# Recurrent scan of a two-layer RWKV and attention network: a new table of hops, finer pieces, a longer pipeline, and the state's identity product in two corners

## The chip, the cores and the metric

The kernel runs on one core of a Trainium2 chip, in one launch. The metric is the device time in microseconds of an execution; lower is better. All arithmetic is in float32; PE is TensorE, DVE is VectorE, ACT is ScalarE, POOL is GpSimd, SP is SyncE.

## The reference, cut to what matters

Two layers over 256 context rows and 256 latent rows of 1024 channels: layer 0 is an RWKV-7 mixer, layer 1 global attention, each between two gated feed-forward halves. The change touches the recurrence of layer 0 alone. It runs over 16 heads of 64 channels, in two directions, first over the context rows and then, from the state reached, over the latent rows:

```python
def rwkv_scan(state0, dd, reverse):
    def step(s, inp):
        r_t, w_t, k_t, v_t, a_t, b_t = inp
        sa = jnp.einsum('bhvk,bhk->bhv', s, a_t)
        s = s * w_t[:, :, None, :] + sa[..., None] * b_t[:, :, None, :] + v_t[..., None] * k_t[:, :, None, :]
        return s, jnp.einsum('bhvk,bhk->bhv', s, r_t)
    xs = tuple(jnp.moveaxis(dd[nm], 1, 0) for nm in ('r', 'decay', 'k', 'v', 'a', 'b'))
    s_fin, ys = lax.scan(step, state0, xs, reverse=reverse)
    return s_fin, jnp.moveaxis(ys, 0, 1)
```

Each direction's `y` is then normalised per head, scaled, gated and added (the readout).

## The kernel before, in words

The program goes through the network stage by stage; weights are split into two float32r parts so that one product becomes three matmuls. Before the scan a features stage writes, for each of eight channel tiles (128 channels, two heads), the scan's inputs to DRAM; the scan (`rwkv_scan`, from L885) reads them back. It works in chunks of 64 rows: four chunks per half (`hf` 0 is the context, 1 the latent rows), eight steps per tile, both directions `d` and both heads `h` side by side.

A tile goes through four generators. `produce` (L930) makes the chunk matrices in pieces: `scores` (products of `bk` and `ar` on PE, masked by DVE at L951), `keys` (transposes of `bk`, evicted by ACT at L991) and `values` (transposes of `v`, evicted by ACT at L974 and L975). What a piece evicts is put on the list `late` and issued one hop later. `solve` (L997) inverts the small triangular blocks on DVE, some forty instructions in a chain; `couple` (L1032) joins the inverses to 64 rows with four rounds of 32*32 products (`first` twice, `third`, `fourth`, each for two halves `hf`), with DVE and ACT moving the results between (`refine`, `turn`, `diagonal`, `corner`). `scan` (L1135) has three hops per step: A forms `rp` (L1149, and L1156 with the state S) and ACT evicts it as `rt` (L1160), with `past` (L1126) adding the state's part of the output; B forms `up` from `rt` (L1167), evicted by ACT in two halves to `uv`; C forms the new state `sp` from an identity product of S (L1175) and the products of `bkt` and `uv` (L1181), which ACT evicts and scales by `pc` (L1186), and the output `yp` (L1192). `readout` (L1204) follows a half.

The order of all this is written out by hand: the instructions of each engine run in the order in which the program issues them, within a hop the running scan first, then tile by tile, the oldest first. The table `plan` (L94) says at which hop t, counted from a tile's own start, each thing is issued. A tile starts every P = 24 hops, so up to three tiles are under way. PIECES gives the hops of the twelve pieces (four scores, four keys, four values), SOLVE the start of the solve and RATE its instructions per hop, COUPLE the couple's hops, SCAN the start of the scan, SS and BC (modulo 24) two parts of the readout, BK the loads of the next tile's `pc`, `ar` and `bk`, V those of the own `v`, LOADS those of `ax` and `r`. All these loads but tile 0's, and the readout's, go through POOL's queue (`ldq`), in program order too, beside POOL's memsets of `uv`.

Buffers: `ar` and `v` come from a pool of two (one per half), `pc` from a pool of three (`m3`), `bkt` and `uv` from one of four; `bk` is two fixed tiles `bks`, `ax` and `tt` two fixed tiles each. A write into a buffer waits for the last read of its last owner, wherever that read stands in the program. `pc` of a tile is read by L1186 in hop C of steps 0 to 6. PSUM banks for pieces, couple and readout come from one pool of five.

The lines that carry the order:

```python
                for z in reversed(live[:]):
                    if hop - z[0] >= pl["SCAN"] and not adv(z[5]):
                        live.remove(z)
```

Of the kernel before, what the change touches and what calls it, by code (L numbers as in the profile page):

```python
# [12 lines left out]
ALU = mybir.AluOpType  # L13
# [74 lines left out]
class Net:  # L88


    def __init__(self, ctx, tc, a):
        self.ctx, self.tc, self.nc, self.a = ctx, tc, tc.nc, a
        self.last = {}
        self.plan = dict(  # L94
            P=24, SOLVE=12, RATE=6, COUPLE=range(24, 32), SCAN=32,
            PIECES=(0, 3, 6, 9, 8, 11, 16, 18, 12, 14, 20, 21),
            END={(0, 0): (5, (3, 3)), (0, 1): (5, (3, 3)), (1, 0): (5, (3, 3))}, WO=(4, 4), NI=(5, 5),
            FST=(1, 3), WAIT=16, RH=0, FB=16, CLEAR=(14, 18), AS=1, BK=(11, 20), V=(5, 13), LOADS=(21, 33), SS=(21, 10), BC=(1, 14))
        nc = self.nc
        self.res = ctx.enter_context(tc.tile_pool(name="res", bufs=1))  # L100
        self.dram = ctx.enter_context(tc.tile_pool(name="dram", bufs=1, space=DRAM))
        self.vec = self.res.tile([128, NV, KT], F32, name="vec")
        self.cst = self.res.tile([128, NC], F32, name="cst")
        self.ones = self.res.tile([128, 128], F32, name="ones")
        cv = self.res.tile([128, KT, 2], F32, name="cv")
        self.cs = self.res.tile([128, KT, 32], F32, name="cs")
        self.mod = [self.res.tile([128, NMOD, KT, 2], F32, name=f"mod{l}") for l in range(2)]
        self.epsn = self.res.tile([128, 1], F32, name="epsn")
        self.epsg = self.res.tile([128, 1], F32, name="epsg")
        self.xsp = self.dram.tile([128, 2, KT, CTX], F32, name="xsp")  # L110
        nc.sync.dma_start(out=cv, in_=a["cv"])
# [773 lines left out]
    def rwkv_scan(self):  # L885
        nc, a, tc = self.nc, self.a, self.tc
        with ExitStack() as st:
# [12 lines left out]
            def load(ct, hf, ldq=nc.gpsimd):  # L900

                z = zs.setdefault(ct, {})
                if hf == 0:
                    z["pc"] = m3.tile([128, 2, 8], F32, tag="pc", name="pc")
                    ldq.dma_start(out=z["pc"], in_=self.fpc[ct])
                z["bk", hf] = bks[hf]
                z["ar", hf] = e2.tile([128, 2, 4, 2, 64], F32, tag="ar", name="ar")
                ldq.dma_start(out=z["ar", hf].rearrange("p d c s i -> p (d c s i)"), in_=self.far[ct, :, hf].rearrange("p d x -> p (d x)"))
                ldq.dma_start(
                    out=bks[hf].rearrange("p d c x -> p (d c x)"), in_=self.fbk[ct, :, hf].rearrange("p c s i -> p (c s i)"))  # L910

            def load_v(ct, hf):
                z = zs[ct]
# [16 lines left out]
            def produce(ct):  # L930
# [4 lines left out]
                def after(f):  # L935

                    late.append(f)

                def scores(hf, d):

                    bk, ar = z["bk", hf], z["ar", hf]
                    p = [psc.tile([128, 4, 128], F32, tag="sc", name="scp") for _ in range(2)]
                    for c in range(4):
                        for h in range(2):
                            q = 64 * h
                            nc.tensor.matmul(  # L946
                                out=p[h][:, c], lhsT=bk[q:q + 64, d, c], rhs=ar[q:q + 64, d, c].rearrange("p s i -> p (s i)"),
                                start=True, stop=True, tile_position=(q, 0))

                    def f(h):  # L950
                        nc.vector.tensor_tensor(out=sc[:, hf, d, :, h], in0=p[h], in1=mask, op=ALU.mult)  # L951
                        if h == 0:
                            after(lambda: f(1))
                    after(lambda: f(0))

                def values(hf, d):

# [21 lines left out]
                def keys(hf, h):  # L979
# [7 lines left out]
                    for d in range(2):  # L987
# [2 lines left out]
                                p[:, d, c], bk[q:q + 64, d, c], idn[q:q + 64, q:q + 64])  # L990
                    after(lambda: nc.scalar.activation(out=bkt[:, :, :, h], in_=p, func=AF.Copy))  # L991

                return [lambda g=g, hf=hf, e=e: g(hf, *e)
                        for g, es in ((scores, ((0,), (1,))), (keys, ((0,), (1,))), (values, ((0,), (1,))))
                        for hf in range(2) for e in es]

            def solve(ct):  # L997

# [6 lines left out]
                for q in range(0, 128, 32):  # L1005
                    src = sca[q:q + 32, :, 1 - q // 64, q % 64:q % 64 + 32]
                    nc.vector.transpose(out=ext[q:q + 32], in_=src.rearrange("p u (j t) -> p t u j", j=2))
                    yield q == 96
                    yield
                xl = m1.tile([128, 16, 16], F32, tag="xl", name="xl")  # L1010
                nc.vector.scalar_tensor_tensor(
                    out=xl, in0=ext[:, :, 0:16], scalar=m[0], in1=ext[:, :, 16:32], op0=ALU.mult, op1=ALU.add)
# [19 lines left out]
            def couple(ct):  # L1032
# [5 lines left out]
                def ublock(u, q, h, c0):  # L1038
                    return z["sc"][q:q + 32, u // 8, u // 4 % 2, u % 4, h, c0:c0 + 32]
# [14 lines left out]
                def half(t, hf):  # L1054
                    return t[:, 8 * hf:8 * hf + 8]
# [2 lines left out]
                qt = m1.tile([128, 16, 32], F32, tag="qt", name="qt")  # L1058
                wd = m1.tile([128, 16, 32], F32, tag="wd", name="wd")
                p = [None, None]  # L1060
                nc.vector.transpose(out=tn, in_=td)
                p[0] = first(0, lambda u, q: ublock(u, q, 1 - q // 64, q % 64), tn)
                yield
                p[1] = first(1, lambda u, q: ublock(u, q, 1 - q // 64, q % 64), tn)
                nc.vector.tensor_tensor(out=half(qt, 0), in0=half(tn, 0), in1=p[0], op=ALU.add)
                yield
                nc.vector.tensor_tensor(out=half(qt, 1), in0=half(tn, 1), in1=p[1], op=ALU.add)
                p[0] = first(0, lambda u, q: qt[q:q + 32, u], td)
                yield
                p[1] = first(1, lambda u, q: qt[q:q + 32, u], td)  # L1070

                def refine(hf):
                    nc.vector.scalar_tensor_tensor(
                        out=half(wd, hf), in0=half(td, hf), scalar=2.0, in1=p[hf], op0=ALU.mult, op1=ALU.subtract)
                    nc.vector.transpose(out=half(tn, hf), in_=half(wd, hf))

                refine(0)
                yield
                refine(1)

                def third(hf):
                    p[hf] = bank()
# [8 lines left out]
                    nc.scalar.activation(out=half(qt, hf)[32:64], in_=p[hf][32:64], func=AF.Copy)  # L1091
                    nc.vector.tensor_copy(out=half(qt, hf)[96:128], in_=p[hf][96:128])

                def diagonal(hf):
                    for q in range(0, 128, 32):
                        nc.scalar.activation(out=tt[q:q + 32, hf, :, q:q + 32], in_=half(wd, hf)[q:q + 32], func=AF.Copy)

                def fourth(hf):
                    p[hf] = bank()
# [7 lines left out]
                def corner(hf):  # L1107
                    nc.scalar.activation(out=tt[64:96, hf, :, 96:128], in_=p[hf][64:96], func=AF.Copy, scale=-1.0)
                    nc.vector.tensor_scalar(out=tt[0:32, hf, :, 32:64], in0=p[hf][0:32], scalar1=-1.0, scalar2=None, op0=ALU.mult)

                third(0)
                third(1)
                yield
                turn(0)
                turn(1)
                diagonal(0)
                yield
                fourth(0)
                fourth(1)
                yield  # L1120
                corner(0)
                corner(1)
                diagonal(1)
                yield

            def past(yp, S, r, c):  # L1126
# [8 lines left out]
            def scan(ct):  # L1135
                z = zs[ct]
                S = None
                for i in range(8):
# [33 lines left out]
                    if i < 7:  # L1172
                        sp = ps_.tile([128, 2, 64], F32, tag="s", name="sp")
                        if S is not None:
                            nc.tensor.matmul(  # L1175
                                out=sp.rearrange("p d e -> p (d e)"), lhsT=idn, rhs=S.rearrange("p d e -> p (d e)"),
                                start=True, stop=False, skip_group_check=True)
                        for d in range(2):
                            for h in range(2):
                                q = 64 * h  # L1180
                                nc.tensor.matmul(  # L1181
                                    out=sp[q:q + 64, d], lhsT=bkt[:, d, c, h], rhs=uv[:, d, c, h], start=S is None and d == 0, stop=True,
                                    tile_position=(0, q), skip_group_check=True)
                        sn = l2.tile([128, 2, 64], F32, tag="S", name="S")
                        for d in range(2):
                            nc.scalar.activation(out=sn[:, d], in_=sp[:, d], func=AF.Copy, scale=z["pc"][:, d, i:i + 1])  # L1186
# [58 lines left out]

            zs, reads = {}, []
            ldq = nc.gpsimd
            tts, bks, axs = [], [], []
            for i in range(2):
                bks.append(e2.tile([128, 2, 4, 128], F32, tag="bk", name="bk"))  # L1250
            for i in range(2):
                tts.append(l2.tile([128, 2, 8, 128], F32, tag="tt", name="tt"))
                axs.append(l2.tile([128, 2, 4, 2, 64], F32, tag="ax", name="ax"))
# [23 lines left out]
            while hop < P * KT or live or reads:  # L1277
# [10 lines left out]
                for t0, c, pr, so, co, sn in live:  # L1288
# [11 lines left out]
                        drain(so)  # L1300
                    if t in pl["COUPLE"]:
                        adv(co)
                    for i in [i for i, at in enumerate(pl["PIECES"]) if at == t]:
                        pr[i]()
                    for hf in range(2):
                        if t == pl["BK"][hf] and c + 1 < KT:
                            load(c + 1, hf)
# [285 lines left out]
```

## Time and profile before

| | us |
|---|---|
| three runs | 2365.75, 2373.47 (median), 2376.3 |
| profiled execution | 2373.17 |
| its span, first to last instruction | 2371.4 |
| stage of the scan in it, from the first loads to the last readout | 752 to 1130 |
| stages before / after it | 752 / 1241 |

The profile is of one execution. Its times count from the first instruction; a group of rows gives busy time, a timeline the start and the duration of each instruction or run of equal instructions, and in brackets how long the engine stood idle before it and which engine's instruction ended that. A PE row counts two instructions for each float32 product. Matmul ends are modelled, so starts are the better measure.

### The profile page before, as it was taken

To read this page: it belongs to the slowest core of one execution; us is meant where nothing else is said; L and a number is where in the kernel's file an instruction comes from. 1 tells how busy PE (TensorE), PEld (TensorE's weight loads), DVE (VectorE), ACT (ScalarE), POOL (GpSimd) and SP (SyncE) were. 2 spreads that over 40 slices of the span, in tenths; PEclk is the share of its full clock that TensorE was granted. 3 is DMA by queue.
4 is the path that set the end of the run, shared out by engine and by line. 5 is a ranking of instruction groups with operands and counts; after the bars stand their busy time and mean duration, and the time that the engine had idled before them with its cause. 6 is when DMAs were issued, how large, how long until landed. Compare 5 with 4: busy or idle time off the path is not lost.

```text
span 2371.4 us, 44667 instructions
## 1 busy us (share of the span) xinstructions
PE 2188.6 (92%) x18452; PEld 1875.9 (79%) x18452; DVE 1517.2 (64%) x2609; ACT 1077.5 (45%) x1944; POOL 182.6 (8%) x273
## 2 busy tenths in 40 slices
PE   7999999888996799898899999999999999998997
PEld 4777889666774688777888788998878898678997
DVE  3798336576886657663699833479983367775554
ACT  3322225445883445454663222464222355555443
POOL 0000000000453223221000000000000000000000
PEclk9999999898998779998999999999999999798999
DMA  7577336442676434332567633567763364103554
GB/s 257 194 220 225 96 105 191 149 133 82 228 249 208 116 96 120 97 96 72 181 205 243 192 98 91 162 190 231 231 209 92 113 177 136 59 12 122 180 180 138
DMA packets 103051, 366.25 MB, mean 154 GB/s; under 512 B 13008, under 2 KB 15424, under 8 KB 100160
## 3 DMA queue, kind: packets, MB, share of 16 engines
q1 hardware_dynamic: 85536, 300.35, 40.7%
q0 software_dynamic: 17312, 63.05, 8.4%
q8 instruction: 145, 2.38, 0.4%
q14 instruction: 58, 0.48, 0.1%
HBM read 330.78 MB, written 32.57 MB: 153 GB/s over the span
## 4 chain that ended last, share of the span: by engine, by line
PE 49%; DVE 11%; issue 6%; ACT 5%; DMA 5%; POOL 1%; DVEq 0%; SPq 0%; ACTq 0%; POOLq 0%
PE h L261 5%; PE h L259 5%; PE h L260 5%; PE yps L261 4%; PE yps L259 4%; PE yps L260 4%; DMA y<-in_modt 3%; DVE junk L213 3%; DVE wlo L252 2%; PE scp L946 2%; PE op L1457 1%; PE cpl L1049 1%; PE sp L1181 1%; DMA fgl<-yx 1%; PE yo L261 1%
## 5 line engine op out<-in xcount | busy, mean ns | idle before, releaser
L251 ACT ACTIVATE whi<-wp 128x1024 fp32r<-128x1024 f32 (+1 forms) x396 | 409.2, 1034 | 738.8 <-PE h L260 389.9
L252 DVE TENSOR_TENSOR wlo<-wp,whi 128x1024 fp32r<-128x1024 f32 (+1 forms) x396 | 471.9, 1192 | 382.5 <-ACT whi L251 378.7
L261 PE MATMUL h<-nh,wlo 128*128 128x512 f32 (+1 forms) x1520 | 525.2, 347 | 18.3 <-DVE wlo L252 18.0
L259 PE MATMUL h<-nh,whi 128*128 128x512 f32 (+1 forms) x1520 | 523.8, 345 | 8.1 <-ACT whi L251 6.3
L260 PE MATMUL h<-nh,whi 128*128 128x512 f32 (+1 forms) x1520 | 522.8, 344 | 0.0
L261 PEld LDWEIGHTS h<-nh,wlo 128*128 128x128 f32 x1520 | 290.0, 191 | 63.2 <-DVE wlo L252 29.4
L259 PEld LDWEIGHTS h<-nh,whi 128*128 128x128 f32 x1520 | 290.4, 191 | 42.1 <-ACT whi L251 7.9
L260 PEld LDWEIGHTS h<-nh,whi 128*128 128x128 f32 x1520 | 290.4, 191 | 33.6
L261 PE MATMUL yps<-hid,wlo 128*128 128x256 f32 (+1 forms) x1034 | 314.2, 304 | 1.9 <-DVE wlo L252 1.9
L259 PE MATMUL yps<-hid,whi 128*128 128x256 f32 (+1 forms) x1034 | 314.2, 304 | 0.0
L260 PE MATMUL yps<-hid,whi 128*128 128x256 f32 (+1 forms) x1034 | 313.9, 304 | 0.0
L261 PEld LDWEIGHTS yps<-hid,wlo 128*128 128x128 f32 x1034 | 197.4, 191 | 10.7 <-DVE wlo L252 2.8
L260 PEld LDWEIGHTS yps<-hid,whi 128*128 128x128 f32 x1034 | 197.5, 191 | 7.9
L259 PEld LDWEIGHTS yps<-hid,whi 128*128 128x128 f32 x1034 | 197.5, 191 | 7.7
L213 DVE SCALAR_TENSOR_TENSOR junk<-y 128x1024 bf16<-128x1024 f32 x144 | 176.1, 1223 | 20.6 <-DMA y<-in_modt 18.6
L404 DVE TENSOR_TENSOR gg<-s,h 128x512 f32<-128x512 f32 (+1 forms) x98 | 56.0, 572 | 95.1 <-PE h L261 93.1
L213 DVE SCALAR_TENSOR_TENSOR junk<-dw,cb 128x1024 bf16<-128x1024 f32 x80 | 97.9, 1224 | 13.5 <-DMA dw<-in_modt 10.2
L406 ACT ACTIVATE hid<-gg 128x512 fp32r<-128x512 f32 (+1 forms) x98 | 52.3, 534 | 111.4 <-DVE gg L404 111.2
L261 PE MATMUL pp<-hid,wlo 128*128 128x512 f32 x232 | 92.5, 400 | 7.0 <-DVE wlo L252 6.8
L259 PE MATMUL pp<-hid,whi 128*128 128x512 f32 x232 | 93.0, 401 | 4.2 <-ACT whi L251 4.2
L260 PE MATMUL pp<-hid,whi 128*128 128x512 f32 x232 | 91.9, 396 | 0.0
L951 DVE TENSOR_TENSOR sc<-scp,cst 128x512 f32<-128x512 f32 x64 | 42.8, 685 | 31.2 <-PE scp L946 31.0
(306 smaller groups left out, 3536.5 us busy)
## 6 DMA issues: line engine op xcount, KB each, us to landing
wp<-in_w SPq DMA_DIRECT2D x243, 512.0 KB, 3.6
wp<-in_w SPq DMA_DIRECT2D x94, 448.0 KB, 3.4
y<-in_modt SPq DMA_DIRECT2D x72, 512.0 KB, 4.4
dw<-in_modt SPq DMA_DIRECT2D x40, 512.0 KB, 4.2
wp<-in_wrkv SPq DMA_DIRECT2D x40, 512.0 KB, 4.0
mw<-in_modw SPq DMA_DIRECT2D x32, 512.0 KB, 4.9
far<-ar POOLq DMA_DIRECT2D x8, 1024.0 KB, 5.9
ar<-far POOLq DMA_DIRECT2D x14, 512.0 KB, 5.0
```

The costliest lines, as they stand in the source:

```text
L213: nc.vector.scalar_tensor_tensor(out=junk, in0=ws[i % len(ws)], scalar=1.0, in1=cb[:, s], op0=ALU.mult, op1=ALU.mult, accum_out=self.mod[l ...
L251: nc.scalar.activation(out=hi, in_=raw, func=AF.Copy)
L252: nc.vector.tensor_tensor(out=lo, in0=raw, in1=hi.bitcast(F32), op=ALU.subtract)
L259: nc.tensor.matmul(out=ps, lhsT=wh, rhs=vh, start=first and j == 0, stop=False)
L260: nc.tensor.matmul(out=ps, lhsT=wh, rhs=vl, start=False, stop=False)
L261: nc.tensor.matmul(out=ps, lhsT=wl, rhs=vh, start=False, stop=last and j == n - 1)
L404: nc.vector.tensor_tensor(out=gg, in0=s1, in1=ps[1], op=ALU.mult)
L406: nc.scalar.activation(out=hi, in_=gg, func=AF.Copy)
L946: nc.tensor.matmul(out=p[h][:, c], lhsT=bk[q:q + 64, d, c], rhs=ar[q:q + 64, d, c].rearrange("p s i -> p (s i)"), start=True, stop=True, t ...
L951: nc.vector.tensor_tensor(out=sc[:, hf, d, :, h], in0=p[h], in1=mask, op=ALU.mult)
L1049: nc.tensor.matmul(out=p[q:q + 32, u], lhsT=lhs(8 * hf + u, q), rhs=rhs[q:q + 32, 8 * hf + u], start=True, stop=True, tile_position=(q, q))
L1181: nc.tensor.matmul(out=sp[q:q + 64, d], lhsT=bkt[:, d, c, h], rhs=uv[:, d, c, h], start=S is None and d == 0, stop=True, tile_position=(0, ...
```

## The change

The plan gets new hops. The pieces are named (`s` scores, `k` keys, `v` values; half, then direction or head; for scores also which two of four chunks) and placed in a table FILL. Scores are cut in two; the couple takes eleven hops where it took eight, with at most one round's half on PE and one `diagonal` copy (now by 32-row strip over both halves, four where there were eight) in each; the scan starts at t = 41 where it started at 32. `bk` comes from the pool of four, and the next tile's loads are issued at t = 6 and 9. The solve yields once per strip transpose. The identity product is issued as two products of 64 rows and 64 columns.

```diff
-            P=24, SOLVE=12, RATE=6, COUPLE=range(24, 32), SCAN=32,
-            PIECES=(0, 3, 6, 9, 8, 11, 16, 18, 12, 14, 20, 21),
+            P=24, SOLVE=14, RATE=5, COUPLE=range(30, 41), SCAN=41,
+            FILL={0: ("s000", "s001"), 1: ("s010",), 2: ("s011",), 3: ("s100", "s101"), 4: ("s110",), 5: ("s111",), 15: ("k00",),
+                  16: ("v00",), 17: ("v01",), 19: ("k01",), 20: ("k10",), 21: ("k11",), 22: ("v10",), 23: ("v11",)},
...
-            FST=(1, 3), WAIT=16, RH=0, FB=16, CLEAR=(14, 18), AS=1, BK=(11, 20), V=(5, 13), LOADS=(21, 33), SS=(21, 10), BC=(1, 14))
+            FST=(1, 3), WAIT=16, RH=0, FB=16, CLEAR=(14, 18), AS=1, BK=(6, 9), V=(8, 14), LOADS=(30, 42), SS=(6, 18), BC=(10, 22))
...
-                z["bk", hf] = bks[hf]
+                z["bk", hf] = m4.tile([128, 2, 4, 128], F32, tag="bk", name="bk")
...
-                    p = [psc.tile([128, 4, 128], F32, tag="sc", name="scp") for _ in range(2)]
-                    for c in range(4):
+                    if part == 0:
+                        z["ps"] = [psc.tile([128, 4, 128], F32, tag="sc", name="scp") for _ in range(2)]
+                    p = z["ps"]
+                    for c in (2 * part, 2 * part + 1):
...
-                def diagonal(hf):
-                    for q in range(0, 128, 32):
-                        nc.scalar.activation(out=tt[q:q + 32, hf, :, q:q + 32], in_=half(wd, hf)[q:q + 32], func=AF.Copy)
+                def diagonal(q):
+                    nc.scalar.activation(
+                        out=tt[q:q + 32].rearrange("p f u t -> p (f u) t")[:, :, q:q + 32], in_=wd[q:q + 32], func=AF.Copy)
...
+                nc.vector.transpose(out=tn, in_=td)
+                yield
+                p[0] = first(0, lambda u, q: ublock(u, q, 1 - q // 64, q % 64), tn)
+                yield
+                p[1] = first(1, lambda u, q: ublock(u, q, 1 - q // 64, q % 64), tn)
+                nc.vector.tensor_tensor(out=half(qt, 0), in0=half(tn, 0), in1=p[0], op=ALU.add)
+                yield
+                p[0] = first(0, lambda u, q: qt[q:q + 32, u], td)
+                nc.vector.tensor_tensor(out=half(qt, 1), in0=half(tn, 1), in1=p[1], op=ALU.add)
+                yield
+                p[1] = first(1, lambda u, q: qt[q:q + 32, u], td)
+                refine(0)
+                yield
                 third(0)
+                refine(1)
+                yield
                 third(1)
                 turn(0)
+                diagonal(0)
+                yield
+                fourth(0)
                 turn(1)
+                diagonal(32)
+                yield
                 fourth(1)
                 corner(0)
+                diagonal(64)
+                yield
                 corner(1)
+                diagonal(96)
                 yield
...
-                            nc.tensor.matmul(
-                                out=sp.rearrange("p d e -> p (d e)"), lhsT=idn, rhs=S.rearrange("p d e -> p (d e)"),
-                                start=True, stop=False, skip_group_check=True)
+                            for q in (0, 64):
+                                nc.tensor.matmul(
+                                    out=sp[q:q + 64].rearrange("p d e -> p (d e)"), lhsT=idn[q:q + 64, q:q + 64],
+                                    rhs=S[q:q + 64].rearrange("p d e -> p (d e)"),
+                                    start=True, stop=False, tile_position=(q, q), skip_group_check=True)
```

## Rows read from the trace of the kernel before

**Rows 1.** Stretches: start:end, length, busy per engine, granted clock, DMA share, GB/s.

```profile
752.00:798.30 46.30, 25.21 (x601) 23.60 (x602) 25.56 (x62) 15.45 (x27) 11.42 (x19) 0.61 0.49 139
798.30:841.80 43.50, 40.47 (x930) 35.22 (x931) 24.92 (x64) 21.15 (x65) 12.86 (x21) 0.81 0.34 101
841.80:887.00 45.20, 41.68 (x948) 36.02 (x947) 27.57 (x70) 21.82 (x68) 12.85 (x21) 0.86 0.36 103
887.00:930.10 43.10, 39.72 (x940) 34.44 (x940) 27.59 (x70) 21.77 (x67) 12.86 (x21) 0.88 0.36 104
930.10:970.00 39.90, 35.72 (x940) 30.71 (x940) 27.67 (x70) 21.81 (x67) 12.86 (x21) 1.00 0.39 118
970.00:1011.40 41.40, 37.55 (x940) 32.27 (x940) 27.35 (x70) 21.80 (x67) 12.85 (x21) 0.96 0.36 106
1011.40:1051.40 40.00, 35.79 (x940) 30.71 (x940) 27.59 (x70) 21.79 (x67) 15.23 (x26) 1.00 0.41 119
1051.40:1094.80 43.40, 36.77 (x884) 31.45 (x884) 24.43 (x65) 21.79 (x67) 7.50 (x11) 0.87 0.29 89
1094.80:1122.20 27.40, 26.33 (x370) 22.00 (x372) 6.20 (x14) 11.27 (x42) 1.27 (x2) 0.77 0.05 17
```

**Rows 2.** Timeline, PE and ACT, at the end of the period that closes at 1051.4.

```profile
1049.21 1.69 ACT L1096 ACTIVATE tt<-wd 32x256 f32<-32x256 f32 x4
...
1049.30 0.71 PE L989 MATMUL btp<-cst,bk 64*128 64x64 f32 x8
...
1051.74 0.45 PE L1167 MATMUL up<-rt,tt 128*64 128x64 f32 x8 [1.73 <-ACT rt L1160]
```

**Rows 3.** Stretches (columns as in rows 1): one early, two around that point.

```profile
830.70:854.60 23.90, 23.84 (x354) 21.32 (x354) 13.15 (x27) 10.82 (x33) 6.66 (x11) 0.50 0.23 70
...
1045.00:1052.60 7.60, 5.39 (x142) 4.61 (x140) 3.85 (x8) 6.46 (x19) 6.15 (x10) 1.00 0.53 154
1052.60:1062.80 10.20, 10.20 (x120) 9.15 (x118) 7.51 (x15) 3.55 (x13) 0.00 (x0) 0.50 0.01 5
```

**Rows 4.** Waits of PE from 798.3 to 1094.8: total us, times, longest.

```profile
PE cpl L1049 <- issue: 4.6, 6, 1.8
```

**Rows 5.** Timeline of PE, 996.8 to 1003.4, at full clock.

```profile
997.47 0.45 PE L1149 MATMUL rp<-uv,sc 128*64 128x64 f32 x8
...
998.08 0.45 PE L1131 MATMUL yp<-r,S 64*64 64x64 f32 x8
998.46 0.72 PE L1049 MATMUL cpl<-td,qt 32*32 32x32 f32 x60
...
1001.11 1.16 PE L946 MATMUL scp<-ar,bk 64*128 64x128 f32 x16
1002.20 0.49 PE L1175 MATMUL sp<-S,cst 128*128 128x128 f32 x2
1002.62 0.45 PE L1181 MATMUL sp<-uv,bkt 128*64 128x64 f32 x8
1002.90 0.40 PE L1192 MATMUL yp<-sc,uv 128*64 128x64 f32 x8
1003.24 0.34 PE L1086 MATMUL cpl<-tn,sc 32*32 32x32 f32 x10
```

**Rows 6.** The page's costliest groups: DVE's masking of the scores.

```profile
L951 DVE TENSOR_TENSOR sc<-scp,cst 128x512 f32<-128x512 f32 x64 | 42.8, 685 | 31.2 <-PE scp L946 31.0
```

**Rows 7.** Timeline of POOL from 926 to 1012, one of six like it.

```profile
964.05 1.39 POOL L924 DMA_DIRECT2D ax<-far  x2 [15.18 <-PE rp L1156]
...
966.30 0.57 POOL L905 DMA_DIRECT2D pc<-fpc  x1
```

**Rows 8.** Timeline of ACT behind rows 5: both evictions of the state.

```profile
1003.18 0.52 ACT L1186 ACTIVATE S<-sp,pc 128x64 f32<-128x64 f32 x2 [2.07 <-PE sp L1181]
```

**Rows 9.** The tile v, 790 to 1060: its loads.

```profile
DMA to landing us min/median/max: 3.2/5.0/6.8
```

**Rows 10.** DMA issues, 851 to 866: KB each, median us to landing.

```profile
v<-fv POOLq DMA_DIRECT2D x2, 256.0 KB, 6.6
```

More of the change, by code (lines that the diff above doesn't have):

```diff
@@ L909, in load @@
                 ldq.dma_start(
-                    out=bks[hf].rearrange("p d c x -> p (d c x)"), in_=self.fbk[ct, :, hf].rearrange("p c s i -> p (c s i)"))
+                    out=z["bk", hf].rearrange("p d c x -> p (d c x)"), in_=self.fbk[ct, :, hf].rearrange("p c s i -> p (c s i)"))
             def load_v(ct, hf):
@@ L937, in after, with scores @@
                     late.append(f)
-                def scores(hf, d):
+                def scores(hf, d, part):
                     bk, ar = z["bk", hf], z["ar", hf]
-                    p = [psc.tile([128, 4, 128], F32, tag="sc", name="scp") for _ in range(2)]
-                    for c in range(4):
+                    if part == 0:
+                        z["ps"] = [psc.tile([128, 4, 128], F32, tag="sc", name="scp") for _ in range(2)]
+                    p = z["ps"]
+                    for c in (2 * part, 2 * part + 1):
                         for h in range(2):
@@ L953, in f @@
                             after(lambda: f(1))
-                    after(lambda: f(0))
+                    if part:
+                        after(lambda: f(0))
                 def values(hf, d):
@@ L991, in keys @@
                     after(lambda: nc.scalar.activation(out=bkt[:, :, :, h], in_=p, func=AF.Copy))
-                return [lambda g=g, hf=hf, e=e: g(hf, *e)
-                        for g, es in ((scores, ((0,), (1,))), (keys, ((0,), (1,))), (values, ((0,), (1,))))
-                        for hf in range(2) for e in es]
+                return lambda nm: dict(s=scores, k=keys, v=values)[nm[0]](*map(int, nm[1:]))
             def solve(ct):
@@ L1007, in solve @@
                     nc.vector.transpose(out=ext[q:q + 32], in_=src.rearrange("p u (j t) -> p t u j", j=2))
-                    yield q == 96
-                    yield
+                    yield True
                 xl = m1.tile([128, 16, 16], F32, tag="xl", name="xl")
@@ L1060, in couple @@
                 p = [None, None]
[L1061 to L1070, printed above, removed]
                 def refine(hf):
@@ L1075, in refine @@
                     nc.vector.transpose(out=half(tn, hf), in_=half(wd, hf))
-                refine(0)
-                yield
-                refine(1)
                 def third(hf):
@@ L1109, in corner @@
                     nc.vector.tensor_scalar(out=tt[0:32, hf, :, 32:64], in0=p[hf][0:32], scalar1=-1.0, scalar2=None, op0=ALU.mult)
+                nc.vector.transpose(out=tn, in_=td)
[11 more added lines that the diff above has]
+                yield
                 third(0)
+                refine(1)
+                yield
                 third(1)
-                yield
                 turn(0)
-                turn(1)
                 diagonal(0)
@@ L1118, in couple @@
                 fourth(0)
+                turn(1)
+                diagonal(32)
+                yield
                 fourth(1)
+                corner(0)
+                diagonal(64)
                 yield
-                corner(0)
                 corner(1)
-                diagonal(1)
+                diagonal(96)
                 yield
@@ L1247, in rwkv_scan @@
             ldq = nc.gpsimd
-            tts, bks, axs = [], [], []
-            for i in range(2):
-                bks.append(e2.tile([128, 2, 4, 128], F32, tag="bk", name="bk"))
+            tts, axs = [], []
             for i in range(2):
@@ L1302, in rwkv_scan @@
                         adv(co)
-                    for i in [i for i, at in enumerate(pl["PIECES"]) if at == t]:
-                        pr[i]()
+                    for nm in pl["FILL"].get(t, ()):
+                        pr(nm)
                     for hf in range(2):
```

## The prediction

> **What bounds the kernel now.** I read the profile from the stage inwards. The only code that changes is the recurrent scan, so first the stretches of its stage, cut at the first `rt` eviction of each of the eight channel tiles [rows 1]. Between one cut and the next lies one period of 24 hops. Seven such periods take 43.5, 45.2, 43.1, 39.9, 41.4, 40.0 and 43.4 us, the last tile's seven steps 27.4, and the lead before the first scan step is 46.3. What to see: two periods ran wholly at a granted clock of 1.00 and took 39.9 and 40.0, with PE busy 35.7 and 35.8; VectorE has 27.6 and ScalarE 21.8, so neither binds over a period. PE's work is the bound, with some 4.2 us of idle on top, and the other periods are longer because the clock stood at half for part of them.
>
> Next, where PE idles: the timeline at the end of a period [rows 2]. ScalarE gets four `diagonal` copies in a row (1.69 us) and the square of the readout, ahead of the `rt` eviction that `up` needs; PE, through with its keys piece at 1050.01, waits 1.73 us. Such a wait, 1.5 to 2.5 us, stands at the end of six periods; the couple's waits on instruction issue make 4.6 us in all [rows 4]. Then what follows it [rows 3]: up to 1052.6 the clock is 1.00, and for the next 10.2 us, with PE busy all the time, 0.50, that is 1.2 instead of 2.4 GHz. Periods with one such stretch took 43.1 and 43.4, against 39.9 and 40.0: 3.2 us each; one that held half of a 24 us stretch of it, with the rest in the period before, took 45.2 [rows 1, 3].
>
> **The change, part by part.** Let t be the hop counted from a tile's own start; the tile before it is at t+24, the one before that at t+48.
>
> *The identity product.* It costs 0.42 us from its start to that of the products behind it, and there are 48 [rows 5]. In two corners it becomes four instructions. The nearest row is `past`, eight instructions in the same two corners (64 rows, half as many columns, twice as many instructions): 0.38 us including the change of shape. I take 0.38: 0.04 x 48 = 2 us less. Ends: half of 0.42 if only the streaming counts (10 us less), 0.60 if the corners take turns, two streams of 0.21 and the change of shape (9 us more). TensorEngine Tiling in the Trainium skill (Restrictions and Gotchas, PSUM Pressure) says that different row tiles cannot access the same PSUM bank simultaneously; by that the corners, which both write the bank of `sp`, would take turns and the sum would be 9 us higher. The row of `past`, whose corners also share a bank, speaks against it: eight products one behind the other would not fit in 0.38 us when eight of 128*64 take 0.28.
>
> *Finer, even pieces.* Two of four score pieces and the third and fourth products of the couple are cut in two: four more changes of shape per tile at about 0.1 to 0.15 (0.38 of `past` against 0.28 of a block followed by its own shape [rows 5]), 0.6 us. The eight `diagonal` copies become four, one a hop, so the lump of 1.69 us goes, and with it the 1.73 us wait. A step of the scan now gets three or four pieces of other PE work, where it had from one to five. Work 35.7 + 0.6 - 0.2 = 36.1 per period; of the idle time I leave 1.1 (0.7 of issue [rows 4], the rest short waits of `sp` on `uv` in hops with a small piece). That gives 37.2 at full clock. Ends: 36.1 with no wait, 40.0 if evenness buys nothing.
>
> *Longer pipeline.* The scan starts nine hops later, but the second tile's four score pieces and its first keys and values move into the lead. VectorE then masks six score banks (0.685 us each [rows 6]) between the first tile's solve and its couple, 4.1 us; PE in turn has no scores inside that couple. I take +3 for the lead (-3 to +6). What moved ahead is missing later: in the seventh period there are no scores, first keys and first values of a ninth tile, some 5.9 us of PE work (four scores at 1.1 [rows 5] with their cuts, two pieces at 0.6); three of its steps then hang on the chain PE, ScalarE, PE, and I take 33.5 (31 to 37) for 43.4. The last tile loses the couple's tail from its first step: -1.5.
>
> Six periods at 37.2 are 223.2 for 253.1 now: -29.9. With -9.9, -1.5 and +3 that is **-38.3 us, if the loads keep up**.
>
> *The loads.* `bk` gets four buffers, so POOL's queue no longer waits there for the keys' transposes. SP's queue loads only tile 0 here and is not passed. But the load of tile c+1 moves from t=11 to t=6, and its first transfer is `pc`, in a pool of three. The buffer it gets is that of tile c-2, whose last read is the S eviction of step 6, at its t = 41+18+2 = 61, tile c's t=13. Before, that was tile c's t=4, ahead of the load: `pc` follows `r` with no wait [rows 7]. Now POOL stands from t=6 to t=13 for c = 2 to 6. POOL takes its instructions in order (`ax` there held everything behind it for 15.18 us [rows 7]), and behind `pc` stand `ar`, `bk`, and then `v` of tile c, which PE wants at t=16. Count from the end of that S. POOL issues `pc`, `ar`, `bk` at about 0.57, so `v` is issued from 1.8 on; it lands 3.2 to 6.8 us after, median 5.0 [rows 9], and 6.6 in a stretch where it followed `bk` [rows 10]. I take 6.0: 7.8. PE gets there sooner. S ends 1.08 us after the start of `sp`'s products [rows 5, 8], by which time PE has done them and `yp` (0.62) and 0.46 of a half piece of the fourth product (0.6); the other 0.14; `rp` with `past` 0.99 and another half piece 0.6; `up` 0.38 and keys 0.71 [rows 2]; `yp` 0.34: 3.2 us. So PE stands 7.8 - 3.2 = **4.6 us** at the first values piece, five times: +23. Ends 1.8 and 5.5 (from 5.0 and 8.7). Queued behind it on PE are the next tile's whole first step, so nothing hides it, but ScalarE and VectorE catch up meanwhile: -1 each time, -5. And a stop of PE at `up` of 1.5 us or more was followed by a stretch at half clock in four of six cases (one of them in [rows 3]); I charge 3.2 for each of the five, +16 (0 to 16).
>
> **The sum.** -38.3 + 23 - 5 + 16 = -4.3. Against the profiled execution's own 2373.17 us this gives 2368.9, said as **2369**; the median of the runs, 2373.47, is 0.3 away. The forecast case is therefore: a real gain in every period, nearly all of it given back at `v`. Its own range is 2350 (wait 1.8, no half clock) to 2385.
>
> **Rivals.** *The wait does not reach PE.* For it: in the kernel before POOL stood at `ax` for 15 us in every period [rows 7] and none of PE's waits from 798.3 on is for a load; and PE's way of 3.2 us to the values piece is longer where ScalarE is late in those hops. Against: `v` lands within 3.2 us of its issue at the very best, and is issued 1.8 late. Then -38.3: 2335.
> *The clock decides, and the kernel is slower.* Place: PE's stop at the values piece. Price: the wait at its upper end of 5.5 with nothing recovered, and half clock as long as in the second period, 45.2 - 40.0 = 5.2. A period is 37.2 + 5.5 + 5.2 = 47.9; five make 239.5 for 213.1, and with -2.8 for the sixth, -9.9, -1.5, +3 that is +15: 2388. It is slower once wait and clock together exceed about 10 us a period.
> *The corners take turns*, by the reading weighed above: +9 on the forecast, 2378. The row of `past` leaves little for it.
> That the change doesn't do what it says (pieces even in the program, uneven on the engines) is the end 40.0 of the period, which lies on the way to the second rival.
>
> **How the numbers follow.** Forecast 0.55, wait hidden 0.22, clock 0.20, corners 0.03. 0.5% is 11.9 us, about what a measurement of this kernel can tell from no change (its three runs span 0.45%): faster is below 2361.6, slower above 2385.3. Of the forecast a third falls below (short waits, full clock), a twentieth above. Faster: 0.22 + 0.18 = 0.40. Slower: 0.15 of the second rival's 0.20, and 0.03: 0.18. The rest, 0.42, is no change. For 8 in 10 the range runs from 2332, below the hidden wait, to 2391, above the clock's price; a faster and a slower case both count, so the forecast's own 2350 to 2385 stands beside it.
>
> **What would show it.** In the changed profile: POOL waiting at `pc` for the S eviction, five times and some 10 us or more each; PE waiting for the load of `v`, five times 2 to 5 us; the 1.73 us wait of `up` gone; periods six and seven near 37 and 33 us, the first five near 43 to 45; the lead near 49; four identity instructions in 0.38 us. The forecast is wrong if PE never waits for `v`, or if the clock stays at 1.00 behind that wait.

## The result: slower by 1.25%, and the profile after

Four runs of the changed kernel took 2392.97 to 2411.39 us, median 2398.51; four runs of the kernel before, three of them those of the table ahead, had a median of 2369.61. The ratio is 1.0125 (95% interval 1.0094 to 1.0157): slower, where 2369 and "no change" were forecast, and above the range's end of 2391. The profiled execution took 2392.97 us (span 2390.3), 19.8 more than that of before; it was the fastest of the four, and no trace shows the 5.5 us between it and the median. From the memset of `eye` to the last `y` of the scan (starts) it is 401.2 against 380.6, 20.6 more: the loss lies in this stage alone.

The stretches between the first `rt` evictions of the tiles, to be held against [rows 1] (columns as there: start:end, length, busy time of PE, PEld, DVE, ACT and POOL, granted clock, DMA share, GB/s):

```profile
798.60:846.30 47.70, 40.31 (x948) 34.55 (x946) 29.77 (x76) 20.86 (x61) 10.83 (x18) 0.82 0.22 69
846.30:894.20 47.90, 41.83 (x958) 35.89 (x957) 27.39 (x70) 21.53 (x63) 12.85 (x22) 0.82 0.32 96
...
990.40:1039.00 48.60, 41.74 (x958) 35.74 (x956) 27.31 (x69) 21.53 (x62) 12.87 (x22) 0.82 0.32 92
1039.00:1077.30 38.30, 36.67 (x968) 31.37 (x964) 23.80 (x64) 21.30 (x63) 11.31 (x19) 0.98 0.35 99
1077.30:1113.50 36.20, 31.90 (x848) 26.56 (x848) 20.44 (x60) 20.38 (x61) 7.06 (x11) 0.95 0.31 89
1113.50:1138.40 24.90, 24.12 (x382) 19.19 (x384) 6.20 (x14) 11.24 (x42) 2.23 (x4) 0.86 0.15 46
```

Five periods of nearly the same 47.7 to 48.6 us, all at a granted clock of 0.82; then one of 38.3 at 0.98 and one of 36.2. At full clock the schedule itself is thus a little better than the old one, whose two periods at 1.00 took 39.9 and 40.0 [rows 1]; something that happens exactly five times eats it. The waits of PE and of POOL from 798 to 1110 name it (total us, times, longest; lines have moved by one to five from those of before):

```profile
PE vtp L973 <- DMA v<-fv: 22.1, 5, 5.1
PE cpl L1050 <- issue: 5.5, 6, 1.2
PE yp L1197 <- ACT uv L1172: 2.8, 6, 0.5
...
PE up L1170 <- ACT rt L1163: 1.2, 2, 0.7
```

```profile
...
POOL pc L906 <- ACT S L1191: 87.7, 5, 18.2
...
```

The old wait of `up` on `rt`, 1.73 us a period [rows 2], is gone (1.2 in all). In its place PE waits five times for the load of `v`, 22.1 us. Behind that stands POOL's wait for the release of `pc`, five times, 87.7 us. One of the five, first in POOL's timeline, then in PE's (start, duration, instruction, in brackets the idle time before it and what ended it):

```profile
933.23 0.56 POOL L906 DMA_DIRECT2D pc<-fpc  x1 [17.53 <-ACT S L1191]
933.78 0.55 POOL L909 DMA_DIRECT2D ar<-far  x1
934.32 0.53 POOL L910 DMA_DIRECT2D bk<-fbk  x1
934.85 0.54 POOL L916 DMA_DIRECT2D v<-fv  x1
```

```profile
934.87 0.71 PE L993 MATMUL btp<-cst,bk 64*128 64x64 f32 x8
936.10 0.74 PE L1197 MATMUL yp<-sc,uv 128*64 128x64 f32 x8 [0.52 <-ACT uv L1172]
940.78 1.12 PE L973 MATMUL vtp<-cst,v 128*64 128x64 f32 x16 [3.94 <-DMA v<-fv]
...
958.33 0.44 PE L1179 MATMUL sp<-S,cst 64*64 64x128 f32 x4
958.69 0.45 PE L1186 MATMUL sp<-uv,bkt 128*64 128x64 f32 x8
```

`pc` goes out as soon as step 6 of the tile that had the buffer before, three tiles back, has evicted its state, `v` 1.6 us later, and PE has it 5.9 us after that; it has been idle since 936.8. The last two lines are the identity product in its corners at full clock: 0.36 us to the next product, for 0.42 [rows 5]. What the idle time brings stands in the stretches around it (columns as above):

```profile
930.00:936.80 6.80, 6.28 (x194) 5.27 (x186) 3.87 (x9) 5.71 (x16) 3.57 (x7) 1.00 0.25 67
936.80:940.80 4.00, 0.06 (x3) 0.02 (x2) 3.91 (x5) 1.68 (x3) 3.83 (x7) 0.69 0.92 292
940.80:955.50 14.70, 14.70 (x170) 12.97 (x172) 6.83 (x32) 5.88 (x17) 3.23 (x6) 0.50 0.54 162
```

The clock is 1.00 up to the wait, falls to its lower level of 1.2 GHz in it and stays there for 14.7 us more with PE busy all the time. In the clock's records that stretch lasts 17.07 us, from 938.3. In the waits of the other tiles begin three of the same length, at 842.8, 890.5 and 986.1, and one of 6.8 at 1033.9. The first period's 0.82 comes mostly from a stretch that the lead left behind, until 812.0.

### The profile page after: what moved, and what is told of

Its sections match the earlier page's. It is cut to its first block, busy times and chain, and to the rows that moved or that the text cites. A ratio compares the mean times of both kernels' runs of the same rounds, so it can differ in the third digit from the quotient of the medians.

```text
span 2390.3 us, 44861 instructions
## 1 busy us (share of the span) xinstructions
PE 2197.2 (92%) x18548; PEld 1880.2 (79%) x18548; DVE 1516.1 (63%) x2609; ACT 1074.1 (45%) x1912; POOL 182.5 (8%) x273
## 4 chain that ended last, share of the span: by engine, by line
PE 47%; DVE 10%; issue 9%; DMA 6%; ACT 3%; POOL 1%; DVEq 0%; ACTq 0%; SPq 0%; POOLq 0%
PE h L262 5%; PE h L260 5%; PE h L261 5%; PE yps L262 4%; PE yps L260 4%; PE yps L261 4%; DMA y<-in_modt 3%; DVE junk L214 3%; DVE wlo L253 2%; DMA v<-fv 1%; PE op L1460 1%; DMA fgl<-yx 1%; PE yo L262 1%; PE vtp L973 1%; PE yo L260 1%
## 5 line engine op out<-in xcount | busy, mean ns | idle before, releaser
L261 PEld LDWEIGHTS h<-nh,whi 128*128 128x128 f32 x1520 | 289.3, 191 | 33.5
L260 PE MATMUL yo<-nh,whi 128*128 128x256 f32 x192 | 56.6, 295 | 6.5 <-ACT nh L252 3.8
```

What stands on the lines that cost most here:

```text
L260: nc.tensor.matmul(out=ps, lhsT=wh, rhs=vh, start=first and j == 0, stop=False)
L261: nc.tensor.matmul(out=ps, lhsT=wh, rhs=vl, start=False, stop=False)
```

## The experiments

Theory after the result: PE stands 4 to 5 us for `v` five times, because `pc`'s pool of three holds POOL up, and the idle time is followed by half clock, which costs as much again. Rivals: the schedule itself costs more than forecast (finer pieces, corners), and the wait is a symptom; or the clock falls whatever PE waits for.

**Take the cause of the wait away: `pc` from a pool of four.**

```diff
-                    z["pc"] = m3.tile([128, 2, 8], F32, tag="pc", name="pc")
+                    z["pc"] = m4.tile([128, 2, 8], F32, tag="pc", name="pc")
```

> The changed kernel with pc from the pool of four. Theory A (the load of v, held behind pc, and the half clock that follows are the whole loss): POOL no longer waits at pc, PE no longer waits for v, the first five periods fall from 48 us to the 38.3 of the sixth, so 5 x 9.8 = 49 us less than the changed kernel: near 2350, some 20 us faster than before. Theory B (the even order and the longer pipeline are themselves slow): within 10 us of the changed kernel's 2398.

Median 2385.66, ratio to the kernel before 1.005 (1.0024 to 1.0077). Both waits are gone, and yet there is no gain over before. The first of its waits of PE, 798 to 1110, then its POOL and its PE at one such place:

```profile
PE cpl L1050 <- issue: 15.7, 7, 5.0
...
```

```profile
855.11 1.39 POOL L925 DMA_DIRECT2D ax<-far  x2 [12.66 <-PE rp L1159]
...
862.14 1.09 POOL L967 MEMSET uv<- 64x512 f32 x2
```

```profile
865.79 0.69 PE L1050 MATMUL cpl<-td,qt 32*32 32x32 f32 x56
871.48 0.33 PE L1050 MATMUL cpl<-td,qt 32*32 32x32 f32 x8 [5.00 <-issue]
```

A new stop has taken the place of the old one: in the couple, in the middle of 64 equal instructions (32 products), PE stands for 5 us and waits for nothing that the profile shows. Between the two POOL lines ten transfers go out in 7 us (`ax`, `r`, `pc`, and twice `ar`, `bk`, `v`): with four buffers of `bk` POOL no longer waits for the keys' transposes, as it does in the kernel with the diagonal copies below (68.5 us in 12 waits). That this lost pacing makes the burst is argued; `bk` back in two buffers was not run. The stretches around it:

```profile
862.30:866.50 4.20, 4.17 (x232) 3.64 (x233) 0.95 (x3) 1.53 (x7) 2.11 (x4) 1.00 0.94 327
866.50:871.50 5.00, 0.02 (x4) 0.02 (x4) 0.00 (x0) 0.49 (x1) 0.00 (x0) 0.81 0.53 197
871.50:880.00 8.50, 8.50 (x242) 7.02 (x243) 3.37 (x8) 2.68 (x9) 0.00 (x0) 0.71 0.02 4
```

327 GB/s of loads, PE at a standstill, then the clock down. Half clock lasts only 6.8 us here, though the stop is as long as the waits for `v`. The longest stretch of this run, 34.1 us from 958.4, begins behind a stop of 2.0. So the length of a stop does not set what follows it; what does is not settled.

The queue table of the page (packets, MB, share) lets one read what PE can have waited for; this is the changed kernel's, then that of the run with four buffers from 866.5 to 871.5, the stop itself:

```profile
...
q8 instruction: 145, 2.38, 0.4%
...
```

```profile
q0 software_dynamic: 302, 0.97, 51.2%
q8 instruction: 1, 0.02, 1.4%
```

145 packets of 16.4 KB. Theory from here: q8 carries PE's instructions, and a burst of loads delays its next packet.

The traces bear it out. Counted over all of PE's instructions (matmuls, weight loads, semaphores), the ten longest stops on issue of this run from 780 to 1100 lie 256, 1280, 2048, 1792, 1792, 256, 1792, 2048 and 1792 instructions apart: multiples of 256 without exception. The stops on issue above 0.8 us of every other run, the kernel before included, leave the same remainder by 256 from the first `rt` to 1095. In the stop above, the one packet of q8 ran from 869.17 to 870.25, 6.8 us after the start of the last, and PE went on at 871.48. PE has 18,548 matmul instructions, as many weight loads and 224 others, 37,320 in all, and 145 packets of 256 hold 37,120: one packet short. The couple's 32*32 products use them up fast: 465 matmuls and weight loads in the 4.2 us before the stop.

The Trainium skill (Runtime: NRT & Kernel Launch, Instruction fetch mechanics) says that a sequencer fetches its instructions itself in blocks of 16 KiB, 256 each, and that crossing a block is mostly hidden. The block's size agrees; that it is hidden does not hold beside 327 GB/s of loads.

**Keep `pc`'s wait, but put both loads of `v` ahead of it.**

```diff
-BK=(6, 9), V=(8, 14)
+BK=(6, 9), V=(5, 5)
```

> The changed kernel with both loads of v issued at t=5, ahead of pc, and pc left in its pool of three. Theory A in its narrow form (only v, among all that stands behind pc, is late): POOL still stands at pc five times for about 17 us, and yet the time is that of the run with four buffers, near 2350. If another load behind pc (ar, bk, ax, r) is late as well, the periods stay above 40 us.

Median 2361.35, ratio 0.996 (0.9933 to 0.9986). No wait of PE for `v` is left, and POOL still stands for `pc`:

```profile
POOL pc L906 <- ACT S L1191: 89.3, 5, 20.0
...
```

That alone shows no price. This is 37 us below the changed kernel. Its periods are 38.1, 38.6, 39.3, 41.7, 43.1, 47.7 and 36.2: the first three, which are at full clock but for the first 2.6 us, take 38 to 39. The 47.7 has 27 us of half clock, of two stretches behind stops on issue of only 1.5 and 1.4; why so much is not settled.

**Keep the wait, and let PE work in it.** Before the first values piece of tiles 2 to 6, five products of 128*128 by 512 into a bank of the pieces' pool are added, which nobody reads; they fill most of the idle time.

```diff
+                        if nm == "v00" and 2 <= c < KT - 1:
+                            w = psc.tile([128, 512], F32, tag="sc", name="fillp")
+                            for _ in range(5):
+                                nc.tensor.matmul(out=w, lhsT=idn, rhs=cst[:, 0:512], start=True, stop=True)
```

> The changed kernel with five products of 128x128 by 128x512 on constants, into a bank that nobody reads, ahead of the first values piece of tiles 2 to 6: PE has some 4.5 us of work while it waits for v. Theory A1 (PE's standing still is what brings the half clock, and it costs 5 us a period): the granted clock stays at 1.00 behind the wait and the five periods fall from 48 to about 43, 2373 in all. Theory A2 (the small pieces behind it bring it, whatever PE did before): half clock as in the changed kernel, periods of 48 or more, 2398.

Median 2366.87, ratio 0.9988 (0.9964 to 1.0013). Two of its periods, columns as above:

```profile
842.00:884.40 42.40, 41.21 (x965) 32.80 (x964) 28.35 (x72) 21.44 (x62) 13.39 (x22) 1.00 0.39 116
884.40:926.80 42.40, 40.31 (x963) 32.30 (x962) 27.64 (x70) 21.44 (x62) 12.99 (x22) 1.00 0.36 108
```

The load is as late as ever and POOL waits as long (86.8 us at `pc`), but the clock stays at 1.00 and a period takes 42.4, on the mean of five too, for 48.1. The pieces behind the wait are the same, so they alone do not bring the half clock. This splits the loss: 42.4 - 38.3 = 4.1 us a period for the wait, 48.1 - 42.4 = 5.7 for the half clock behind it. Work that does nothing bought 31.6 us.

**Is it the corners?** `pc` from four, and the identity product whole again, as it was before.

> The run with four buffers of pc, with the identity product whole again (128x128). By the rows, 0.42 us instead of 0.37 for 48 of them: 2.4 us more PE work, and at most that in the time, 2350 to 2353. If the corners matter beyond that (the clock, a wait on the way to S), 5 us or more.

Median 2370.7, ratio 1.0006 (0.9982 to 1.003), 15 us below the same kernel with corners. The corners' own 48 products differ by 0.06 us each, 3 us in all, so most of it is no price of theirs. The couple's stops on issue are as long (17.1 us in six, longest 4.7) but fall in other places, and half clock takes 54 us of the seven periods for 100; why is not shown. So I tried the corners by themselves, in a kernel without those stops (below).

**Place the loads.** First `pc` from four, with the second half of the next tile's loads late and `v` early; then `pc` from three again and both halves late.

```diff
-BK=(6, 9), V=(8, 14)
+BK=(7, 19), V=(3, 4)
...
-BK=(6, 9), V=(8, 14)
+BK=(19, 20), V=(3, 4)
```

> The run with four buffers of pc, its loads spread: both v at t=3 and 4, the first half of the next tile's ar and bk at t=7, the second at t=19, each behind another wait of POOL's queue, so that some 1.5 MB come at once instead of 3. The same bytes, the same order of work. Theory C (a burst of loads holds up PE's own instruction fetch): the waits of PE on issue of 4 to 5 us in the couple fall below 1.5, half clock behind them with it, all periods come to 38 to 39, and the time to 2335 to 2345. Theory D (those waits are PE's rate of instructions in the 32x32 products, whatever the loads do): they stay at 4 to 5 us, 2385 as in the run with four buffers.

> The changed kernel with pc in its pool of three and no buffer more: v at t=3 and 4, both loads of the next tile at t=19 and 20, behind the second wait at ax and past the last read of pc's old owner. POOL never waits at pc, PE never for v; but ar and bk of both halves, 2 MB, come in one burst behind ax and r. Theory C: waits on issue of 1 to 3 us, between the paced run and the one with four buffers, 2345 to 2365. Theory D: as the run with four buffers, 2385.

The first: 2364.56, ratio 0.9971 (0.9945 to 0.9997), where 2335 to 2345 were expected; its profiled execution took 2374.45. The couple's stops on issue fell to 1.7 us at the longest (2.1 at `up`), yet from 798 to 1110 the mean granted clock was 0.82:

```profile
798.00:1110.00 312.00, 290.06 (x6632) 247.63 (x6630) 179.99 (x459) 150.48 (x438) 83.30 (x133) 0.82 0.30 93
```

Of the loads, `ax`, `r`, `pc`, `ar` and `bk` of the first half still go out together, just ahead of the couple. Why the clock stays low with stops this short (a stretch of 30.7 us begins at the end of one of 1.7, at 951.5) is not settled. In the kernel before, too, the longest stretch, 23.9 us from 830.7, begins behind a stop on issue of 1.8 [rows 3, 4].

The second: 2352.93, ratio 0.9937 (0.9914 to 0.996), with the loads beside the keys and values instead. Of its stretch from 835 to 960:

```profile
835.00:960.00 125.00, 114.48 (x3068) 97.45 (x3063) 87.55 (x221) 71.75 (x205) 43.17 (x71) 1.00 0.37 115
```

Full clock for 125 us; the first four periods take 37.8, 38.3, 39.5 and 39.2. The changed schedule with its loads at other hops is 46 us faster than as it was made.

**Only the diagonal copies, in the kernel before.** Eight copies become four, one a hop; the couple gets a ninth hop.

```diff
-COUPLE=range(24, 32), SCAN=32,
+COUPLE=range(24, 33), SCAN=32,
...
-                def diagonal(hf):
-                    for q in range(0, 128, 32):
-                        nc.scalar.activation(out=tt[q:q + 32, hf, :, q:q + 32], in_=half(wd, hf)[q:q + 32], func=AF.Copy)
+                def diagonal(q):
+                    nc.scalar.activation(
+                        out=tt[q:q + 32].rearrange("p f u t -> p (f u) t")[:, :, q:q + 32], in_=wd[q:q + 32], func=AF.Copy)
...
```

> The kernel before with its eight diagonal copies made four, one a hop, the couple one hop longer, nothing else. If the lump of ACT is what stops PE for 1.7 us at the end of a period and brings the half clock behind it: that wait goes, five periods lose 1.7 and those with half clock 3.2 more, 15 to 20 us less than before: 2350 to 2356. If another eviction takes its place on ACT: within 6 us of before.

Median 2348.61, ratio 0.9913 (0.988 to 0.9947): the lowest median of all. The stretch in which the kernel before went through the seven periods of [rows 1]:

```profile
798.30:1094.80 296.50, 272.19 (x6800) 232.50 (x6800) 190.68 (x487) 155.04 (x464) 88.32 (x143) 0.97 0.36 107
```

Its periods are 38.6 to 40.8 us, for 39.9 to 45.2 before, and the mean clock is 0.97. The wait at the period's end falls from 1.73 to 0.6 at most in the first six periods, and nearly all of the half clock goes with it. The time cannot be told from that of finer pieces, corners and longer pipeline together with the loads placed well: the intervals of the two ratios overlap.

**The corners, in that kernel.** The diff of the identity product alone, added to the one above.

> The kernel before with the four diagonal copies (2348.6 us in the run of it alone) and, added, the state's identity product in two corners. Theory: the corners themselves are worth the 0.05 us that the rows show (0.42 to 0.37), 48 times, 2.4 us: 2346, and the identity rows show 0.36 to 0.37. Rival (the corners' extra instructions and changes of shape cost what the rows at one place don't show): 2350 to 2358.

Median 2352.11, ratio 0.993 (0.9904 to 0.9957), beside 0.9913 (0.988 to 0.9947) without: the intervals overlap, so a gain or a loss of 2 us can't be told. The row shows 0.37 us.

**Do loads stop PE's instructions?** The kernel with the diagonal copies, in which no wait on issue after the first step is above 1.4 us, gets four loads of 512 KB that nobody reads, for each of tiles 1 to 5. First on SP's queue, at t = 25 and at t = 14:

```diff
+                    if t == 25 and 1 <= c < KT - 2:
+                        for i in range(4):
+                            nc.sync.dma_start(out=extra[i], in_=self.fbk[i, :, 0].rearrange("p c s i -> p (c s i)"))
```

> The kernel before with the four diagonal copies, and at t = 25, inside the couple of tiles 1 to 5, four loads of 512 KB that nobody reads, on SP's queue (2 MB, five times). Theory (a burst of loads during the couple holds up PE's instructions): PE stops on issue in the couple, 2 to 5 us each of five times, and where it does a half-clock stretch follows: 5 x 2 to 5 x 10 us over 2348.6, so 2358 to 2398, and the issue waits of PE's couple go from 3.0 us in all to 10 to 25. Rival (loads and PE's instructions don't meet; the stops came from elsewhere): 2347 to 2352, issue waits near 3.

> As the burst in the couple, but the same 2 MB at t = 14, beside the keys and values pieces of the tile, for tiles 1 to 5. Theory (what counts is where the burst lies: the couple's short products use up instructions fastest): no stop of 2 us on issue, or one or two; the own loads of bk and v land later, by up to 7 us, and v's first half is read at t = 12 and was issued at t = 5, so it is in time, its second at t = 20, issued at t = 13, some 11 us before: 2348 to 2360. Rival (a burst anywhere holds up PE alike): as much as the burst in the couple costs.

2362.57, ratio 0.9973 (0.9953 to 0.9993), and 2361.55, ratio 0.9963 (0.9938 to 0.9989). Neither put its loads where it was meant to: nothing held SP, so all twenty, 10 MB, went out in the lead, both times. That makes them two runs of another experiment, on the first tile's couple. The wait of PE on issue there, in the kernel without extra loads (timeline), then with those of t = 25 and of t = 14 (waits up to 815):

```profile
787.12 0.65 PE L1049 MATMUL cpl<-td,qt 32*32 32x32 f32 x31 [1.12 <-issue]
```

```profile
PE cpl L1049 <- issue: 6.5, 1, 6.5
```

```profile
PE cpl L1049 <- issue: 6.1, 1, 6.1
```

The same instructions, and nothing changed but loads that no engine waits for: 1.1 us became 6.5 and 6.1. All three stops stand at one place in the program and leave the remainder by 256 of those above. In both runs with the loads PE went on 1.3 to 1.4 us after the end of a packet of q8. The lead grew from 49.5 to 54.4 and 54.5 us (the first tile's `v` also lands later in both). So the loads do it. The medians rose by 13 to 14 us; the traces show no more than the lead's 5, and the seven periods took 275.3 and 273.5 for 274.8.

Then the same two in POOL's queue (`ldq` for `nc.sync`), which waits in order and so keeps them in their periods:

> On SP's queue nothing held the extra loads: all twenty went out at once in the lead, both times, beside the first tile's couple. Here they stand in POOL's queue at t = 25, behind the tile's own ax, which POOL gets to at about t = 28: 2 MB beside the couple of each of tiles 1 to 5. Theory: PE stops on issue there, 2 to 6 us in most of the five, with half clock behind: 2358 to 2395, issue waits of the couple 10 to 25 us between the first step and the last tile. Rival: only the lead's 10 MB matter, 2 MB are too few: 2347 to 2354, and no stop above 2 us.

> The same 2 MB at t = 14 in POOL's queue, beside the keys and values pieces and ahead of nothing that PE wants within 20 us but v's second half, issued at t = 13. Theory: no stop of 2 us on issue in the couple, 2347 to 2360. Rival (a burst anywhere holds up PE's instructions): stops of 2 us and more at keys, values or score lines, and as much time as the burst beside the couple.

2375.64, ratio 1.0013 (0.9992 to 1.0035), and 2371.36, ratio 1.0004 (0.9975 to 1.0033): 2 MB a period undo the whole gain of the diagonal copies, at either hop. Waits on issue came back, up to 3.1 us in the first and 4.7 in the second. That the hop decides is therefore not shown. The second, around its longest stop (columns as above):

```profile
855.00:860.00 5.00, 4.65 (x100) 4.05 (x96) 3.87 (x13) 3.28 (x11) 2.87 (x4) 1.00 1.03 395
860.00:865.30 5.30, 4.51 (x168) 3.72 (x164) 1.89 (x4) 2.80 (x9) 1.27 (x2) 1.00 1.03 199
865.30:870.00 4.70, 0.02 (x2) 0.00 (x0) 0.00 (x0) 0.00 (x0) 0.00 (x0) 0.67 0.23 78
```

The extra loads went out at 847.6, yet the DMA engines were full until 865: the tile's own `ax`, `r` and `v` queued behind them. The stop again falls in the couple, and a burst at any hop before it seems to do, as long as its backlog reaches that far. A burst that provably ends before the couple was not tried.

## Why the prediction was wrong

The mechanism was the one predicted, to the place and the number; its price was not, and so the wrong case was called the likeliest.

- *The wait at `v`* (4.6 us, five times): right. It measured 5.07, 4.81, 3.94, 4.32 and 3.94, and POOL's wait for the S eviction of step 6 stood behind it, as worked out from the pool of three.
- *What follows the wait* (half clock 3.2, recovery -1): here the forecast failed. A period with the wait took 48.1 on the mean of five, the sixth without it 38.3; less 4.4 of wait, 5.4 are left where 2.2 were charged: 16 us over five. The 3.2 was the difference that a stretch of about 10 us made [rows 1, 3]; in these waits began stretches of 17 us, four times in five, and of 6.8 the fifth time, while the first period pays for the lead's instead. By the microsecond the charge was right: 3.2 for 10.2 us of half clock is 0.31, 5.4 for 17.07 is 0.32. The length was wrong, and with it the price. Of the recovery of 1 at most 0.3 showed: with PE kept at work a wait of 4.4 still cost 4.1. The longer stretch stood in the rows (23.9 us, 12.8 of them in the second period), and its 5.2 had been given to a rival at 0.20. That rival had the mechanism and the direction; that its period of 47.9 is so near the 48.1 is partly luck, for its full-clock period was 1.1 too short and its wait 1.1 too long.
- *The period at full clock* (37.2): 38.3, nearer the middle of its ends 36.1 and 40.0; 1.1 in each of six, 6.6 us. PE was busy 36.7 for 36.1, some of it at half clock (the clock came back 1.7 us into this period), and idle 1.6 for 1.1.
- *The seventh period* (33.5): 36.2 at a clock of 0.95, +2.7. *The lead* (+3): from the memset of `eye` to the first `rt` 53.5 for 49.2, +4.3. *The last tile* (-1.5): -2.5.
- *The identity product* (0.38 us): 0.36 to 0.37. That the corners take turns, at 0.60, is excluded; the rule of TensorEngine Tiling in the Trainium skill (Restrictions and Gotchas, PSUM Pressure), by which they would, doesn't show here.
- The sum of these differences, 16 for the clock, -1 for the shorter wait, 6.6, 2.7, 1.3 and -1, is 24.6; the forecast was 24 below the profiled execution's 2393, and 30 below the median.

"The wait does not reach PE" was put at 2335. Without the wait at `v` the runs gave 2352.9 to 2385.7, because of a second limit, of which the rows of before show only 4.6 us of the couple's waits on issue in all [rows 4]: the loads come in bursts that hold up PE's own instructions, and half clock comes with it. The stops are explained; the half clock of these runs, 18 to 116 us in the seven periods, is not.

## What to carry to other kernels

A stop of PE has two prices, its length and the half clock behind it. The second was 17 us long behind some stops of 4 us and 3.4 behind others, so charge a range that reaches to the longest stretch in the rows of before, and not the mildest case. When a load is moved earlier, look for the oldest buffer that it has to get, and at what stands behind it in its queue; when a buffer is added, ask which loads it had been pacing. And try the smallest part of a large change alone: four copies where there were eight gave as much as all the rest did, as far as the intervals tell.

## What the runs showed of the hardware

Loads that nobody waits for can stop TensorE: with 200 to 400 GB/s of them, PE stood 4 to 6.5 us in the middle of a run of equal 32*32 products. Such stops fall at whole multiples of 256 of its instructions, and PE goes on 1.2 to 1.5 us after a packet of its instruction queue.

In waits of 4 to 5 us for `v` the granted clock fell to 1.2 GHz and stayed there for 17 us four times in five, although PE was busy throughout again; products that nobody reads, issued in the wait, kept it at 2.4. That length is not fixed: behind the scan's stops on issue of 3.5 to 5.0 us (runs with `pc` from four) it was 3.4 to 6.8, and behind some of 1.3 to 2.1 it was 14 to 34. What decides it is not shown.
